# The delta rule's substitution columns: from SBUF to a PSUM bank

## The chip, the cores and the metric

The kernel runs on one core of one Trainium2 chip. The metric is the device time of one execution in microseconds, from the first to the last instruction, and less is better. Five engines work on their own instruction queues and wait for each other by semaphores: TensorE (PE), VectorE (DVE), ScalarE (ACT), GpSimd (POOL) and SyncE (SP), which issues most transfers. PE's results go to PSUM, eight banks of 512 fp32 words on each of 128 partitions. SBUF is the large working memory, and weights come from HBM.

## What is computed

The reference is a model of two layers on 512 tokens of width 1024. Each layer has a mixer and an expert stage (32 experts, two for each token). The first layer's mixer holds a linear recurrence and gated linear attention; the second layer's mixer, where the change lies, is a gated delta rule with eight heads of width 128. Its core is a triangular solve for each chunk, which is then followed by a recurrence over the chunks:

```
decay = exp(where(incl, gcum[:, None] - gcum[None, :], -inf))
k_beta = k * beta
lower = where(strict, einsum('id,jd->ij', k_beta, k) * decay, 0)
rhs = concat([v * beta, k_beta * exp(gcum)])
sol = triangular_solve(lower, rhs, unit_diagonal=True)
u, w = split(sol)
# recurrence: v_new = u - w @ state; o = q' @ state + att @ v_new
```

The reference takes chunks of 64 tokens. The kernel takes blocks of 128 tokens and builds the inverse of each unit lower triangular matrix once.

## The kernel before

**Stages.** One program runs through the first layer's mixer, its expert stage, the second layer's mixer (about 810 to 1215 us of the span) and its expert stage. In the mixers PE multiplies activations by weight blocks of 1 MB. Each weight block is split into a rounded part (`whi`, by ACT, L423) and a rest (`wlo`, by POOL, L424), and three products (L430 to L432) go into one bank of PSUM.

**The mixer with the delta rule** (`mixer_c`). The eight heads go in four groups of two. For each group, units "k", "q", "v" and "z" are projected; the units "o" are output projections. Each projected unit goes on by itself, as a generator that gives way for a number of steps: `keys` convolves (L1013, three DVE instructions on a PSUM bank and an SBUF tile), applies Silu on ACT (L1014), turns the result with PE, and makes the decay-weighted products `LT` (L1064). `queries` sums squares (POOL `sq` L1073, DVE `xt` L278 and `xr` L280, PE L284) and multiplies (L1082, L1083). `values` turns and scales (L1095, L1097).

**The solve.** When both heads of a group have their keys, `solve` starts. Its first part inverts all 32x32 diagonal blocks of the group at once, and it is the part that is touched. ACT gathers the blocks (`Ld`, four copies, L1107), DVE transposes them so that each partition holds one matrix (`Ll`, L1109) and scales them (L1112). `Yl` starts as a copy of the unit columns `y0` (L1114, POOL), which are made once. Then come 31 steps, each with one product and one difference on DVE: `tm = Yl column x Ll column` (L1119) and `Yl = Yl - tm` (L1121). Each difference needs the product before it and each product needs the difference before it, so the 62 instructions are one chain; they have 8 to 76 elements per partition. At the end `Yl` is transposed back into `Yt` (L1123), from which `X` (ACT, L1130) and `XT` (DVE, L1129) are filled. After a number of steps the blocks are joined with PE (L1138 to L1165), and `recurrence` (L1185 to L1213) uses the inverse.

**Order.** A planner behind the program sorts each engine's queue by the order of the program and by the time at which it reckons an instruction can start, so the substitution's instructions lie between convolutions, scalings and the recurrence's instructions on DVE. Each queue then runs in order. Tiles of PSUM come from one pool of eight (`ps`, one bank each), and a tile is given back when its last reader is done. `Yl` has one buffer of its own in SBUF (`ep`, `bufs=1`), so a group's copy waits for the group before.

Of the kernel before, what the change touches and what calls it, by code (L numbers as in the profile page):

```python
# [7 lines left out]
F32 = mybir.dt.float32  # L8
# [3 lines left out]
AF = mybir.ActivationFunctionType  # L12
# [5 lines left out]
P = 128  # L18
# [71 lines left out]
class Build:  # L90
# [829 lines left out]
    def mixer_c(self, u, es, right, second):  # L920
        tc, nc, a, st = self.tc, self.nc, self.a, self.stream
        C = self.C
        ep = self.pool(es, "ce")
# [18 lines left out]
        y0 = ep.tile([P, 8, 32], F32, name="y0")  # L942
# [80 lines left out]
        def keys(h, hd, p, g):  # L1023
# [43 lines left out]
            if g.nk == HG:  # L1067
                st.spawn(solve(g), 0)
# [31 lines left out]
        def solve(g):  # L1100


            LT = g.LT
            sb = [slice(32 * b, 32 * b + 32) for b in range(4)]
            Ld = ep.tile([P, 32, U], F32, name="Ld", bufs=1)
            for b in range(4):
                nc.scalar.activation(Ld[sb[b]], LT[sb[b], :, sb[b]].rearrange("p u i -> p i u"), AF.Copy)  # L1107
            Ll = ep.tile([P, 32, 32], F32, name="Ll", bufs=1)
            nc.vector.transpose(Ll.rearrange("p i j -> p (i j)"), Ld[:, :, None, :].to_broadcast([P, 32, 4, U]))  # L1109
            sl = ep.tile([P, 32], F32, name="sl", bufs=1)  # L1110
            nc.vector.transpose(sl, g.s[:, None, :].to_broadcast([P, 4, U]))
            nc.vector.tensor_mul(Ll, Ll, sl[:, :, None].to_broadcast([P, 32, 32]))  # L1112
            Yl = ep.tile([P, 8, 32], F32, name="Yl", bufs=1)
            nc.gpsimd.tensor_copy(Yl, y0)  # L1114
            tm = wk.tile([P, 256], F32, name="ltmp", tag="Pm", bufs=1)
            for s in range(31):
                n, c = 31 - s, s // 4 + 1
                tv = tm[:, :c * n].rearrange("l (c r) -> l c r", r=n)
                nc.vector.tensor_mul(tv, Yl[:, :c, s:s + 1].to_broadcast([P, c, n]),  # L1119
                                     Ll[:, s + 1:, s].rearrange("p (o r) -> p o r", o=1).to_broadcast([P, c, n]))  # L1120
                nc.vector.tensor_sub(Yl[:, :c, s + 1:], Yl[:, :c, s + 1:], tv)  # L1121
            Yt = ep.tile([P, 32, U], F32, name="Yt", bufs=1)
            nc.vector.transpose(Yt.rearrange("p c u -> p (c u)"), Yl.rearrange("p c r -> p (c r)"))  # L1123
            yield g.wait
            while g.i > self.solved:
                yield 1
            for b in range(4):
                src = Yt[sb[b]].rearrange("p c u -> p u c")
                nc.vector.transpose(XT[sb[b], :, sb[b]], src)  # L1129
                nc.scalar.activation(X[sb[b], :, sb[b]], src, AF.Copy)  # L1130
            yield 1

            lo32 = slice(0, 32)
            pP = self.ps([P, U, 32])
            for i in range(U):
                for b in range(2):
                    lo, hi = slice(64 * b, 64 * b + 32), slice(64 * b + 32, 64 * b + 64)
                    nc.tensor.matmul(pP[hi, i], LT[lo, i, hi], X[lo, i, lo], start=True, stop=True)  # L1138
            Pm = wk.tile([P, U, 64], F32, name="Pm", tag="Pm", bufs=1)
            for b in range(2):  # L1140
                hi = slice(64 * b + 32, 64 * b + 64)
                nc.vector.tensor_mul(Pm[hi, :, lo32], pP[hi], g.s[hi, :, None].to_broadcast([32, U, 32]))
            yield 2
            pX = self.ps([P, U, 32])
            for i in range(U):
                for b in range(2):
                    lo, hi = slice(64 * b, 64 * b + 32), slice(64 * b + 32, 64 * b + 64)
                    nc.tensor.matmul(pX[hi, i], XT[hi, i, hi], Pm[hi, i, lo32], start=True, stop=True)
                    nc.tensor.matmul(pX[lo, i], Pm[hi, i, lo32], XT[hi, i, hi], start=True, stop=True)
            for b in range(2):  # L1150
                lo, hi = slice(64 * b, 64 * b + 32), slice(64 * b + 32, 64 * b + 64)
                nc.vector.tensor_scalar(X[hi, :, lo], pX[hi], -1.0, None, op0=OP.mult)
                nc.scalar.activation(XT[lo, :, hi], pX[lo], AF.Copy, scale=-1.0)
            yield 2

            lo, hi = slice(0, 64), slice(64, 128)
            pP = self.ps([P, U, 64])
            for i in range(U):
                nc.tensor.matmul(pP[hi, i], LT[lo, i, hi], X[lo, i, lo], start=True, stop=True)
            nc.vector.tensor_mul(Pm[hi], pP[hi], g.s[hi, :, None].to_broadcast([64, U, 64]))  # L1160
            yield 2
            pX = self.ps([P, U, 64])
            for i in range(U):
                nc.tensor.matmul(pX[lo, i], Pm[hi, i], XT[hi, i, hi], start=True, stop=True)
            nc.scalar.activation(XT[lo, :, hi], pX[lo], AF.Copy, scale=-1.0)  # L1165
            if g.i == 0:
                self.dump("XT", XT)
            yield 2
            yield from recurrence(g)
            self.solved += 1  # L1170
# [817 lines left out]
```

## Time and profile before

| | |
|---|---|
| median of 3 runs | 1734.37 us (1732.44 to 1738.6) |
| the profiled execution | 1732.64 us, its span 1730.8 us |
| PE busy | 1636.0 us, 95% |
| PE's weight loads (beside PE) | 980.7 us, 57% |
| DVE busy | 797.8 us, 46% |
| ACT busy | 520.9 us, 30% |
| POOL busy | 397.2 us, 23% |
| mean transfer rate over the span | 286 GB/s read from HBM, of which the expert stages' main parts reach 413 GB/s |
| mean granted TensorE clock | 0.975 |

Busy shares are means over stages with different limits, so the page alone doesn't say what bounds the mixer with the delta rule. For that the trace is asked by stretch: who waited for whom, which instructions ran in order of time on each engine, and how long one instruction of a line took at least, at the median and at most. An instruction that takes much longer than others of its own shape was held by something while it ran.

### The profile page before, as it was taken

The page shows a single profiled execution, that of the slowest core. Times are in us where ns is not written, and L with a number is a line of the kernel's source. Part 1 is how long each engine was busy: PE and PEld are TensorE (multiplying, and loading weights), DVE is VectorE, ACT ScalarE, POOL GpSimd, SP SyncE. Part 2 cuts the span into 40 slices and gives each one's busy share as a digit, 9 for nine tenths or more (in the row PEclk, how much of TensorE's full clock was granted, in tenths as well). Part 3 has the DMA queues.
Part 4 walks back from the last instruction along what each step waited for, and adds up shares of the span by engine and source line. Part 5 has one row for each costly group of instructions (what it writes and reads, how often), then busy time and mean ns, then how long its engine had stood idle before and what let it go on. Part 6 is the DMA issues. An engine that isn't in the chain of part 4 may idle for free. (4 is left out here: it accounts for less than half of the span.)

```text
span 1730.8 us, 23035 instructions
## 1 busy us (share of the span) xinstructions
PE 1636.0 (95%) x8890; PEld 980.7 (57%) x8890; DVE 797.8 (46%) x1770; ACT 520.9 (30%) x1029; POOL 397.2 (23%) x350
## 2 busy tenths in 40 slices
PE   6999998899999999998988989899899999999996
PEld 3666667444455455454666666678544555455453
DVE  3346452433324243325688687865433324243324
ACT  4755323210111111015636466364310111111013
POOL 2454432210101001011434343453210001001011
PEclk9999998999999999998999999999999999999998
DMA  8665745689999999994243433136699999999992
GB/s 302 225 222 169 268 147 189 269 343 380 414 411 413 412 411 414 412 407 122 73 145 114 134 98 116 55 139 252 252 379 383 414 411 413 412 412 413 412 406 101
DMA packets 156561, 496.02 MB, mean 287 GB/s; under 512 B 16472, under 2 KB 43668, under 8 KB 141088
## 3 DMA queue, kind: packets, MB, share of 16 engines
q1 hardware_dynamic: 155488, 493.23, 74.1%
q8 instruction: 72, 1.18, 0.3%
q10 hardware_dynamic: 960, 1.28, 0.2%
q14 instruction: 41, 0.34, 0.1%
HBM read 492.21 MB, written 2.10 MB: 286 GB/s over the span
## 5 line engine op out<-in xcount | busy, mean ns | idle before, releaser
L1530 PE MATMUL ps<-w,XTm 128*64 128x512 f32 x2048 | 447.1, 593 | 0.6 <-DVE XTm L1459 0.6
L1530 PEld LDWEIGHTS ps<-w,XTm 128*64 128x64 f32 x2048 | 161.6, 137 | 268.3 <-issue 260.0
L424 POOL TENSOR_TENSOR wlo<-w,whi 128x512 fp32r<-128x512 f32 x136 | 184.6, 1363 | 243.8 <-ACT whi L423 224.9
L1584 PE MATMUL ps<-w,hT 128*64 128x512 f32 (+1 forms) x1056 | 230.8, 587 | 1.0 <-ACT hT L1562 1.0
L1553 DVE TENSOR_TENSOR gg<-gg,ps 128x512 f32<-128x512 f32 x32 | 22.0, 688 | 377.8 <-PE ps L1530 377.7
L430 PE MATMUL ps<-w,whi 128*128 128x512 f32 x384 | 165.0, 430 | 0.0
L431 PE MATMUL ps<-w,whi 128*128 128x512 f32 x384 | 155.5, 405 | 1.6 <-POOL w L554 1.2
L1584 PEld LDWEIGHTS ps<-w,hT 128*64 128x64 f32 x1056 | 82.2, 137 | 130.1 <-issue 117.4
L432 PE MATMUL ps<-w,wlo 128*128 128x512 f32 x384 | 155.8, 406 | 0.0
L1607 DVE TENSOR_TENSOR w<-w,ps 128x512 f32<-128x512 f32 (+1 forms) x248 | 149.2, 662 | 7.0 <-PE ps L1598 5.5
L1539 POOL CAST sel<-ident 32x128 fp32r<-32x128 f32 x32 | 9.0, 280 | 591.3 <-PE ps L1567 533.9
L1588 POOL TENSOR_TENSOR yl<-y,yh 128x512 fp32r<-128x512 f32 x60 | 76.5, 1275 | 251.2 <-ACT yh L1587 251.2
L1587 ACT ACTIVATE yh<-y 128x512 fp32r<-128x512 f32 (+1 forms) x66 | 40.8, 618 | 295.2 <-DVE y L1586 294.2
L423 ACT ACTIVATE whi<-w 128x512 fp32r<-128x512 f32 x136 | 84.5, 627 | 140.2 <-PE ps L431 69.1
L1454 PE MATMUL ps<-Dm,hhi 128*128 128x256 f32 x512 | 125.5, 287 | 0.0
L1454 PE MATMUL ps<-Dm,hlo 128*128 128x256 f32 x512 | 123.4, 283 | 0.0
L1586 DVE SCALAR_TENSOR_TENSOR y<-ps,wsl,gate 128x512 f32<-128x512 f32 (+1 forms) x66 | 48.5, 734 | 151.1 <-issue 76.4
L1454 PEld LDWEIGHTS ps<-Dm,hhi 128*128 128x128 f32 x512 | 101.1, 198 | 13.5 <-issue 13.4
L1598 PE MATMUL ps<-yh,dt 128*128 128x512 f32 (+1 forms) x264 | 106.0, 406 | 0.0
L1562 ACT ACTIVATE hT<-ps 128x512 f32<-128x512 f32 x32 | 19.1, 598 | 284.5 <-PE ps L1560 275.4
L1454 PEld LDWEIGHTS ps<-Dm,hlo 128*128 128x128 f32 x512 | 101.2, 198 | 0.0
L1598 PE MATMUL ps<-yl,dt 128*128 128x512 f32 (+1 forms) x264 | 100.9, 387 | 0.0
(522 smaller groups left out, 2383.5 us busy)
## 6 DMA issues: line engine op xcount, KB each, us to landing
w<-in_moe_w_dram SPq DMA_DIRECT2D x380, 1024.0 KB
w<-in_w_ada_dram SPq DMA_DIRECT2D x40, 1024.0 KB
w<-in_w_in_c_dram SPq DMA_DIRECT2D x16, 1024.0 KB
w<-in_w_in_ab_dram SPq DMA_DIRECT2D x10, 1024.0 KB
wst<-in_w_ada_dram SPq DMA_DIRECT2D x8, 1024.0 KB
w<-in_w_out_ab_dram SPq DMA_DIRECT2D x4, 1024.0 KB
w<-in_moe_w_dram SPq DMA_DIRECT2D x8, 512.0 KB
w<-in_w_out_c_dram SPq DMA_DIRECT2D x4, 1024.0 KB
```

The source lines that it names most:

```text
L423: nc.scalar.activation(hi, src, AF.Copy)
L424: nc.gpsimd.tensor_sub(lo, src, hi.bitcast(F32))
L430: mm(p, lhs[0], rhs[0], start=start, stop=False)
L431: mm(p, lhs[0], rhs[1], start=False, stop=False)
L432: mm(p, lhs[1], rhs[0], start=False, stop=stop)
L1454: nc.tensor.matmul(p, spread(src[:, t], k // 4)[k % 4], Dm[:, t].rearrange("p e s -> p (e s)"), start=t + i == 0, stop=t == NT - 1 and i == 1)
L1530: self.nc.tensor.matmul(ps[j][half[e]], X[:, k, half[e]], w, start=k == 0, stop=k == KD - 1)
L1584: nc.tensor.matmul(py[half[e]], hT[:, k, half[e]], w, start=k == 0, stop=k == 3)
L1586: nc.vector.scalar_tensor_tensor(y32, py, wsl, gate[:, c], op0=OP.mult, op1=OP.mult)
L1588: (nc.vector if last else nc.gpsimd).tensor_sub(yl[:, c], y32, yh[:, c].bitcast(F32))
L1598: mm = nc.tensor.matmul(p, dt[:, t * P:(t + 1) * P], y[:, s], start=i == 0, stop=i == 1)
L1607: nc.vector.tensor_add(h, h, p)
```

## The change

`Yl` becomes a tile of the PSUM pool, and its first content is written by ACT instead of POOL. All later instructions stay as they are in the code, but read and write `Yl` in PSUM.

```diff
             nc.vector.transpose(sl, g.s[:, None, :].to_broadcast([P, 4, U]))
             nc.vector.tensor_mul(Ll, Ll, sl[:, :, None].to_broadcast([P, 32, 32]))
-            Yl = ep.tile([P, 8, 32], F32, name="Yl", bufs=1)
-            nc.gpsimd.tensor_copy(Yl, y0)
+
+            Yl = self.ps([P, 8, 32])
+            nc.scalar.activation(Yl, y0, AF.Copy)
             tm = wk.tile([P, 256], F32, name="ltmp", tag="Pm", bufs=1)
             for s in range(31):
                 n, c = 31 - s, s // 4 + 1
```

`self.ps` takes a whole bank of 512 words and gives a view of the first 256.

## Rows read from the trace of the kernel before

**Rows 1.** The page, part 1: busy us, share of the span, instructions.
```profile
PE 1636.0 (95%) x8890; PEld 980.7 (57%) x8890; DVE 797.8 (46%) x1770; ACT 520.9 (30%) x1029; POOL 397.2 (23%) x350
```

**Rows 2.** PE's waits, 860 to 1135 us: us in total, times, longest.
```profile
PE ps L284 <- DVE xr L280: 5.2, 3, 3.3
PE ps L1095 <- ACT vT L1014: 5.1, 3, 3.2
PE ps L284 <- DVE Yl L1121: 3.1, 1, 3.1
...
PE ps L1029 <- ACT kT L1014: 2.8, 1, 2.8
```

**Rows 3.** Groups by line, 780 to 1200 us: busy us, mean ns | idle before.
```profile
L1119 DVE TENSOR_TENSOR ltmp<-Yl,Ll 128x60 f32<-128x60 f32 (+24 forms) x124 | 44.2, 356 | 2.5
L1121 DVE TENSOR_TENSOR Yl<-Yl,ltmp 128x60 f32<-128x60 f32 (+24 forms) x124 | 41.2, 332 | 2.5
```

**Rows 4.** Single lines, whole span: ns min/median/max, first to last start.
```profile
L1119 DVE TENSOR_TENSOR ltmp<-Yl,Ll x124: 163/265/1396, 867.8 to 1127.0; 128x60 f32<-128x60 f32 x12, 128x28 f32<-128x28 f32 x8, 128x54 f32<-128x54 f32 x8, 128x48 f32<-128x48 f32 x8
L1121 DVE TENSOR_TENSOR Yl<-Yl,ltmp x124: 155/215/1335, 868.1 to 1128.1; 128x60 f32<-128x60 f32 x12, 128x28 f32<-128x28 f32 x8, 128x54 f32<-128x54 f32 x8, 128x48 f32<-128x48 f32 x8
L1064 DVE TENSOR_TENSOR LT<-ps,E x8: 675/685/693, 854.5 to 1085.1; 128x512 f32<-128x512 f32 x8
L1045 DVE TENSOR_TENSOR ksc<-brk,ex x8: 151/976/978, 850.6 to 1083.0; 128x4 f32<-128x4 f32 x8
L1114 POOL COPY Yl<-y x4: 396/397/397, 815.7 to 1057.3; 128x256 f32<-128x256 f32 x4
L1000 DVE COPY ex<-ps x1: 182/182/182, 842.8 to 842.8; 128x32 f32<-128x32 f32 x1
L989 DVE COPY gd<-gd x1: 180/180/180, 840.7 to 840.7; 128x32 f32<-128x32 f32 x1
L1038 PE MATMUL ps<-grow,pick x8: 490/494/792, 846.0 to 1075.3; 40*128 40x512 f32 x8
```

**Rows 5.** DVE's timeline in the first group: start us, us, instruction.
```profile
868.75 1.00 DVE L1119 TENSOR_TENSOR ltmp<-Yl,Ll 128x29 f32<-128x29 f32 x1
869.79 1.18 DVE L1121 TENSOR_TENSOR Yl<-Yl,ltmp 128x29 f32<-128x29 f32 x1
871.00 1.20 DVE L1119 TENSOR_TENSOR ltmp<-Yl,Ll 128x28 f32<-128x28 f32 x1
...
872.34 0.70 DVE L278 STREAM_TRANSPOSE xt<-sq 128x512 f32<-128x512 f32 x1
```

**Rows 6.** POOL's timeline in the same stretch; three instructions, the first and last here.
```profile
868.65 1.04 POOL L1073 TENSOR_TENSOR sq<-qT 128x512 f32<-128x512 f32 x1 [1.95 <-ACT qT L1014]
...
870.88 1.26 POOL L424 TENSOR_TENSOR wlo<-w,whi 128x512 fp32r<-128x512 f32 x1
```

**Rows 7.** The expert stage by windows: PE, PEld, DVE, ACT, POOL, PEclk, DMA, GB/s.
```profile
1400.00:1500.00 100.00, 100.00 (x518) 52.83 (x518) 34.48 (x62) 11.89 (x20) 8.79 (x10) 1.00 1.02 413
```

**Rows 8.** ACT's groups by line and shape, 780 to 1200 us.
```profile
L916 ACT ACTIVATE ychi<-yf 128x256 fp32r<-128x256 f32 x16 | 6.6, 414 | 21.4 <-DVE yf L915 21.4
...
L1053 ACT ACTIVATE E<-E 128x512 f32<-128x512 f32 x8 | 5.0, 626 | 0.0
L1056 ACT ACTIVATE qg<-ps 128x512 f32<-128x512 f32 x8 | 4.7, 591 | 0.1
```

**Rows 9.** Five windows of PE at a low clock: us, busy, PEclk, DMA, GB/s.
```profile
873.40:880.20 6.80, 6.28 (x22) 0.50 0.29 111
...
sum 20.40, PE 19.63; mean PE 3.93
```

**Rows 10.** Timelines in the third group: two output tiles' first matmuls, the last reader.
```profile
1016.48 0.48 PE L430 MATMUL ps<-whi,ychi 128*128 128x512 f32 x1
...
1022.49 0.73 PE L430 MATMUL ps<-whi,ychi 128*128 128x512 f32 x2
...
1034.69 0.68 DVE L530 TENSOR_TENSOR w<-w,ps 128x512 f32<-128x512 f32 x1
```

## The prediction

> **What bounds the kernel now.** The profiled execution took 1732.64 us, of which its span is 1730.8; the median of the three runs, 1734.37, lies 1.7 above it. I read the busy times first: PE is busy for 95% of the span [rows 1]. So a change to DVE counts only where PE waits for DVE. The touched code runs between 868 and 1128 us, in the delta rule of the second layer. I therefore read PE's waits from 860 to 1135 us [rows 2]. The reader is to see two things there. No wait is for a PSUM bank: each names a producer. And all but the weight transfer (2.8), the split on POOL (0.6) and two ACT results (qT 1.0, XT 0.6) end in a DVE result, or in an ACT result (vT, kT) made right behind DVE convolutions. These waits sum to 22.0 us, in twelve rows of which the first four stand here; the other eight have 0.2 to 1.4 each.
>
> Next I asked why DVE is late there. The substitution is 124 products (L1119) and 124 differences (L1121), 85.4 us in all [rows 3]. Their means are 356 and 332 ns, but their medians are 265 and 215 ns [rows 4], so a few are very long. The timeline shows which: an instruction on 29 elements takes 1.00 us, the next two 1.18 and 1.20, just while POOL runs three tensor products back to back [rows 5, 6]. Counted row by row against the shortest of the same shape, 37 of the 248 are longer by more than 0.15 us, and each of the 37 overlaps a POOL instruction. The excess is 7.1, 5.8, 7.6 and 9.3 us in the four groups, 29.8 us together; means less medians give nearly that, 124 x (91 + 117) ns = 25.8 us.
>
> Which DVE instructions are held? One that takes one tensor from PSUM and one from SBUF is not: LT (L1064) on 512 elements spans 675 to 693 ns [rows 4]. One that takes both from SBUF is: ksc (L1045), on 4 elements, is 151 ns at best and 976 at the median [rows 4]. Today all 248 are of the second kind. With Yl in PSUM, each product reads Yl from PSUM and Ll from SBUF, each difference Yl from PSUM and ltmp from SBUF: all become the first kind.
>
> [...]
>
> After 1230 us the expert stage keeps PE busy 100 us of 100 while the transfers run at 413 GB/s [rows 7]. Its loads wait for room that the mixer's last PE and POOL work frees, so I let time saved in the mixer move the end one for one.
>
> **The change part by part.** *POOL loses four copies* of 397 ns [rows 4]. POOL sits idle before nearly all of its work, so I count nothing; if they matter it is a gain of at most 1.6 us. POOL's queue no longer stands behind a copy that waits for the previous group's result.
>
> *ACT gains four copies* into PSUM. An ACT activation on 128x256 takes 414 ns [rows 8]; the table need not change, since the same function already runs between the others. The input y0 has been there since 815 us, so nothing new is waited for but a bank. The cover is the 2.5 us in which DVE transposes and scales Ll behind ACT's Ld. Cost zero; uncovered, 4 x 0.41 = 1.7 us. Behind the copy on ACT stand splits of weights (whi) and Silu; PE would wait for those if the copy waited long for a bank.
>
> *The price of PSUM per DVE instruction.* Reading it costs nothing visible: a copy of 32 elements out of PSUM takes 182 ns, one out of SBUF 180 [rows 4]. No DVE instruction of the trace writes PSUM, and none reads and writes the same bank. I bound it by rows that are far: ACT reading 512 elements from PSUM needs 591 ns against 626 from SBUF [rows 8], so -35 ns; and the product costs 50 ns more than the difference (265 against 215 ns at the median [rows 4]), an access less regular by a stride, so +50 ns. I take +10, nearest to the two copies. On 248 instructions that is 2.5 us of DVE, between -8.7 and +12.4.
>
> [...]
>
> *What PE gets back.* The single waits are read off PE's timeline; their sums by cause are [rows 2]. For each I followed DVE back to its last idle moment and summed the excess on the way; a wait shrinks by no more than that.
> First group: waits 3.15 (L284) and 0.6 (vT). Excess 2.83 before the first, 7.1 before the second. xt (872.34) can't start before POOL's sq ends, 868.65 + 1.04 = 869.69 [rows 5, 6], so 2.6 + 0.6 = 3.2 us.
> Second group: five waits, 1.05 + 0.51 + 1.49 + 1.16 + 0.24 = 4.45 us, against 3.33 of excess: 3.3 us.
> Third group: 3.30 + 0.59, against 3.2: 3.0 us, the same limit by sq. Later the kT wait, 2.75, against 4.05: 2.75 us.
> Fourth group: 1.29 + 3.25 + 1.44 + 0.37 = 6.35, against 8.5: 6.3 us.
> Sum 18.6; about 145 instructions lie in these chains, at +10 ns 1.5 us, of which 0.6 bind: 18.
>
> *The clock.* [...] Since residues of 0.6 to 1 us stay in the first and third groups I take 8.
>
> *What it costs.* Yl holds one of eight banks from its copy to Yt, 25 to 36 us in each group. In groups one, two and four I count, tile by tile from first matmul to last reader, at most six live banks; there it is free. In the third, four outputs of the output projection wait from 1016.5 to 1022.8 us for DVE, and the last is read at 1034.69 [rows 10]. Together with recurrence tiles that makes seven or eight live banks for 8.8 us, all eight for 3.9. One less costs PE between 0 and 8.8 us, and DVE, faster by then, drains earlier: I take 2. If copies were pulled ahead as far as POOL's are (35 to 54 us), banks would be gone twice as long. Against that, eight matmuls (L1038) that lacked only a bank were issued in pairs over 229 us, not at once [rows 4].
>
> *What is late next:* sq on POOL, the w_ada load (2.55 us at 975.6, longer if PE comes earlier), and whatever another order of the queues makes late. I take 4 us.
>
> Sum: 18 + 8 - 2 - 4 = 20 us less. 1730.8 - 20 + 1.84 = 1712.6 for the profiled kind of run, **1714** for the median.
>
> **The rivals.** *A fixed price at the upper bound, +50 ns.* The chains then give 2.9 + 1.7 + 2.4 + 2.2 + 4.9 = 14 us, the clock some 5, less 6: 13, so 1721. Its upside twin, no residue anywhere, gives 21.7 + 9.8 = 31.5: 1703.
>
> *The banks eat it.* The third group loses all 8.8 us and a fall of the clock, 3.4: 20 + 2 - 12 = 10 us gained, 1724. For it: [rows 10]. Against it: PE has other work whose banks are taken already.
>
> *The change doesn't do what it says:* DVE is still held, by what it writes or by Ll alone. Gain 0, banks cost 2: 1736. Against it stand the eight LT rows without a single long one.
>
> *Slower: writing PSUM in a dependent chain.* Every difference waits for the product before it and every product for the difference. If a result in PSUM shows late to the next instruction, each step pays. It decides at 29.8 us / 248 = 120 ns per instruction, where the excess is paid back. At 200 ns DVE gets 49.6 us longer and 19.8 net; by the chains above, +1.3 in group four (49 x 0.2 - 8.5), +3.3 for kT, +3.3 in group two, some 3 in group one, 11 in all: 1745. For it: no row of before prices such a write. Against it: the reads cost 2 ns.
>
> **How the numbers follow.** Forecast 1714, with chance 0.50; the fixed price (1721) 0.20; no residue (1703) 0.05; banks (1724) 0.07; no effect (1736) 0.08; slow writes (1745) 0.10. A measurement of this kernel tells 0.3%, 5.2 us, from no change. Faster by more than that would be 0.82, from the first four; I move 0.02 of it to no change, for orders of the queues that I can't see, and 0.02 to slower, for banks held long. So faster 0.78, same 0.08 + 0.02 = 0.10, slower 0.10 + 0.02 = 0.12. The range reaches from no residue to no effect, 1702 to 1738, and leaves out slow writes and the tails, under 0.2.
>
> **What would show it.** In the changed profile L1119 and L1121 should have no instruction over 0.45 us while POOL runs, and their sum should fall from 85.4 to about 58 us. That sum being above 85 means slow writes; long ones among the 248 still overlapping POOL mean no effect. PE's waits for xr, Yl, kT, vT and vb should fall from some 14 us to 4, and the stretches at 0.50 near 873, 1034, 1064, 1112 and 1119 us should mostly be gone. A PE wait ended by a DVE reader of a bank (L530, L1013), or an ACT wait before the Yl copy, means banks. The expert stage should look the same, only earlier. If DVE is freed by 25 us and the mixer still ends where it did, my step from DVE to PE is wrong.

## The result and the profile after

The change took the time from 1735.69 us (median of six runs) to 1716.22 us, a ratio of 0.9885 with the interval 0.9868 to 0.9902. The forecast was 1714, in a range of 1702 to 1738. The profiled execution of the changed kernel took 1716.33 us and its span 1714.6, against 1732.64 and 1730.8: 16.2 us of span to be found. In the new file every line behind L1114 has moved by one: the product is L1120, the difference L1122, ACT's copy L1115.

First the page, part 1 (busy us, share of the span, instructions), to set beside [rows 1]:

```profile
PE 1630.9 (95%) x8890; PEld 979.8 (57%) x8890; DVE 766.4 (45%) x1770; ACT 522.6 (30%) x1033; POOL 396.1 (23%) x346
```

DVE lost 31.4 us of busy time with the same 1770 instructions. Here are the groups by line, as in [rows 3]:

```profile
L1120 DVE TENSOR_TENSOR ltmp<-ps,Ll 128x60 f32<-128x60 f32 (+24 forms) x124 | 29.3, 236 | 2.4
L1122 DVE TENSOR_TENSOR ps<-ps,ltmp 128x60 f32<-128x60 f32 (+24 forms) x124 | 26.5, 214 | 2.3
```

And the single lines (ns min/median/max, first to last start), as in [rows 4]:

```profile
L1120 DVE TENSOR_TENSOR ltmp<-ps,Ll x124: 154/245/297, 868.7 to 1109.0; 128x60 f32<-128x60 f32 x12, 128x28 f32<-128x28 f32 x8, 128x54 f32<-128x54 f32 x8, 128x48 f32<-128x48 f32 x8
L1122 DVE TENSOR_TENSOR ps<-ps,ltmp x124: 163/218/246, 868.9 to 1109.4; 128x60 f32<-128x60 f32 x12, 128x28 f32<-128x28 f32 x8, 128x54 f32<-128x54 f32 x8, 128x48 f32<-128x48 f32 x8
...
L1115 ACT ACTIVATE ps<-y x4: 361/370/388, 856.3 to 1072.5; 128x256 f32<-128x256 f32 x4
```

The reader is to look at the maxima. 1396 and 1335 ns have become 297 and 246; the sum of the 248 instructions is 55.8 us where it was 85.4. The medians hardly moved: 245 against 265, and 218 against 215. So nothing got faster; the long ones went. The stretch of [rows 5, 6] shows it best, DVE's timeline first and POOL's behind it (start, length):

```profile
869.36 0.20 DVE L1122 TENSOR_TENSOR ps<-ps,ltmp 128x30 f32<-128x30 f32 x1
869.59 0.20 DVE L1120 TENSOR_TENSOR ltmp<-ps,Ll 128x29 f32<-128x29 f32 x1
869.83 0.20 DVE L1122 TENSOR_TENSOR ps<-ps,ltmp 128x29 f32<-128x29 f32 x1
870.56 0.71 DVE L278 STREAM_TRANSPOSE xt<-sq 128x512 f32<-128x512 f32 x1 [0.54 <-POOL sq L1073]
```

```profile
869.49 1.04 POOL L1073 TENSOR_TENSOR sq<-qT 128x512 f32<-128x512 f32 x1 [1.95 <-ACT qT L1014]
870.49 1.28 POOL L1079 TENSOR_TENSOR qg<-qg,qT 128x512 f32<-128x512 f32 x1
871.72 1.29 POOL L424 TENSOR_TENSOR wlo<-w,whi 128x512 fp32r<-128x512 f32 x1
```

The same POOL product sq runs, and beside it the instructions on 29 elements that took 1.00 and 1.18 us now take 0.20 each. In the whole trace 105 of the 248 lie beside a POOL instruction and none is over 0.3 us; before, 61 did, and 37 of them were over 0.45 us. What such an instruction waits for is seen in the trace of before: each of the 37 started while a POOL instruction ran, and ended 0.02 to 0.16 us after that POOL instruction did (in [rows 5, 6], sq ends at 869.69 and the first long one at 869.75; wlo at 872.14 and the third at 872.20). Of the 24 that were not held, 19 had started before the POOL instruction beside them. So these holds lasted as long as what was left of POOL's instruction, to within 0.16 us. The bracket in DVE's fourth line is the new limit: xt waits for sq itself.

PE's waits from 860 to 1135 us (us in total, times, longest), to set beside [rows 2], all that have 0.5 or more:

```profile
PE ps L284 <- DVE xr L280: 3.7, 5, 1.2
PE ps L911 <- ACT orow L907: 2.4, 2, 1.9
PE ps L1139 <- ACT X L1131: 2.3, 2, 2.0
PE ps L1195 <- DVE rr__7207 L1188: 1.6, 1, 1.6
PE ps L258 <- DMA w<-in_w_ada_dram: 1.1, 2, 0.8
PE ps L1186 <- DVE w L530: 1.0, 2, 0.8
PE ps L1195 <- DVE rr__7294 L1188: 1.0, 1, 1.0
PE ps L1082 <- ACT qT L1014: 1.0, 1, 1.0
PE ps L303 <- DMA modst<-modrow: 0.8, 1, 0.8
```

The waits for vT (5.1), Yl (3.1), kT (2.8) and vb (1.4) are gone. But new ones have come: L911 for orow, L1139 for X, L1186 for a bank that DVE (L530) frees, and 0.8 us at L303 for a transfer (modst). All of PE's waits in this stretch came to 27.0 us before and come to 16.6 now, 10.4 less. The clock: six stretches at 0.50 (23.9 us; five are in [rows 9], the sixth is the first line here) have become three (13.6 us, the lines behind it), by windows (length, PE busy, PEld, DVE, ACT, POOL, granted clock, DMA, GB/s):

```profile
975.80:979.20 3.40, 3.40 (x14) 1.57 (x7) 0.79 (x3) 1.21 (x3) 1.98 (x2) 0.50 0.20 26
```

```profile
1021.90:1028.70 6.80, 6.04 (x19) 4.87 (x19) 5.15 (x23) 0.78 (x3) 0.01 (x1) 0.50 0.03 8
1062.80:1066.20 3.40, 3.40 (x13) 1.02 (x9) 1.12 (x2) 2.54 (x8) 1.28 (x1) 0.50 0.22 31
1127.70:1131.10 3.40, 3.40 (x12) 2.71 (x11) 0.83 (x3) 1.76 (x8) 1.56 (x2) 0.50 0.00 0
```

Half of the 10.3 us less at 0.50 is 5.1 us, an estimate from the granted shares of 0.50 and 1.00, and so is each half of such a time below. In the trace of before, matmuls on 512 columns (L430 to L432) that follow each other without idle time start 427 ns apart at 0.50 and 232 at 1.00 (medians; 978.24 and 978.67 us, against 968.19 and 968.42), which would make it 4.7. With the waits the half gives 15.5 of the 16.2 us. From the start of the last norm's warm-up matmuls to the end the two traces are alike, 513.8 and 513.7 us: what the mixer gains moves the end one for one.

### The profile page after: what moved, and what is told of

Same layout as the page of the kernel before. It is cut to its first block, busy times and chain, and to the rows that moved or that the text cites. A ratio compares the mean times of both kernels' runs of the same rounds, so it can differ in the third digit from the quotient of the medians.

```text
span 1714.6 us, 23030 instructions
## 1 busy us (share of the span) xinstructions
PE 1630.9 (95%) x8890; PEld 979.8 (57%) x8890; DVE 766.4 (45%) x1770; ACT 522.6 (30%) x1033; POOL 396.1 (23%) x346
## 3 DMA queue, kind: packets, MB, share of 16 engines
q8 instruction: 72, 1.18, 0.3%
## 5 line engine op out<-in xcount | busy, mean ns | idle before, releaser
L430 PE MATMUL ps<-w,whi 128*128 128x512 f32 x384 | 162.9, 425 | 0.7 <-ACT w L552 0.7
L432 PE MATMUL ps<-w,wlo 128*128 128x512 f32 x384 | 154.1, 402 | 0.0
```

What stands on the lines that cost most here:

```text
L430: mm(p, lhs[0], rhs[0], start=start, stop=False)
L432: mm(p, lhs[1], rhs[0], start=False, stop=stop)
```

## The experiments

The theory: a DVE instruction that reads two SBUF tensors is held while POOL runs a tensor instruction; Yl in PSUM leaves each of the 248 with one SBUF input; the freed DVE time reaches PE as shorter waits and as a clock that doesn't fall. Its rivals: the copy's move from POOL to ACT does it; or the order of the engines' queues, which the planner makes anew for every program (by the lists of both orders, 109 of DVE's 1139 instructions there stand elsewhere in the changed kernel; an expectation below says 64 places); or DVE's mere busy time counts, not the holds; and the bank costs something.

**The copy alone.** Yl stays in SBUF, ACT copies.

```diff
-            nc.gpsimd.tensor_copy(Yl, y0)
+            nc.scalar.activation(Yl, y0, AF.Copy)
```

> Yl stays in SBUF; only its first copy moves from POOL to ACT. If the gain of the change comes from DVE instructions that no longer read two SBUF tensors (theory 1), all 248 are still held: the sum of products and differences stays near 85 us and the time near 1735 us (ratio to before 0.998 to 1.002). If the gain comes from POOL's queue losing its copies, or from another order of the queues (theory 2), the time falls to about 1716 to 1725 us with the sum still near 85.

Measured: 1736.35 us, ratio 0.9997 [0.9986, 1.0009]; the substitution takes 84.8 us. The move of the copy is worth nothing.

**Half of the change, the other tensor.** ltmp goes to PSUM, Yl stays in SBUF: the products still read two SBUF tensors, the differences one.

```diff
-            tm = wk.tile([P, 256], F32, name="ltmp", tag="Pm", bufs=1)
+            tm = self.ps([P, 256])
```

> Yl stays in SBUF with its POOL copy; ltmp goes to a PSUM bank instead, held for as long as Yl's was. The products still read two SBUF tensors, the differences read one from SBUF and one from PSUM. Theory 1: products keep their long instructions (mean about 356 ns, longest about 1.4 us), differences lose theirs (mean about 215, longest under 0.3 us). The excess of before is 11 to 15 us in the differences, so DVE gets 11 to 15 us back and the time falls by about half of the change's 19: 1723 to 1729 us. If a write to PSUM or a bank were what helps or costs (theory 3), products, which write PSUM here, would change as much as differences.

Measured: 1738.79 us, ratio 1.0014 [1.0005, 1.0023]. The single lines:

```profile
L1119 DVE TENSOR_TENSOR ps<-Yl,Ll x124: 174/274/1361, 867.6 to 1118.6; 128x60 f32<-128x60 f32 x12, 128x28 f32<-128x28 f32 x8, 128x54 f32<-128x54 f32 x8, 128x48 f32<-128x48 f32 x8
L1121 DVE TENSOR_TENSOR Yl<-Yl,ps x124: 145/206/235, 867.8 to 1118.8; 128x60 f32<-128x60 f32 x12, 128x28 f32<-128x28 f32 x8, 128x54 f32<-128x54 f32 x8, 128x48 f32<-128x48 f32 x8
```

The mechanism came out as expected: products up to 1361 ns, differences never above 235, 73.4 us in all. What counts here is the inputs: the products, with two from SBUF, are held though they write PSUM. But the time did not follow, and PE has single waits of 8.7 us for vT, 6.0 for rr and 5.2 for Yl, where none was over 3.3 before. The expectation failed. Either freed DVE time is worth nothing here, or something else changed with it. The queues had: ltmp no longer shares its buffer with Pm, and their order is another. So the order had to be held fixed.

**The order of e2 without its tensor in PSUM.** The file of before, its instructions queued on PE, DVE, ACT and POOL in e2's order. Here and below the order is given as a list for each engine, each instruction queued behind the one ahead of it in the list:

```diff
         Build(tc, args, outs[0]).build()
+        fix_order(nc, tc, ORDER)
```

> The kernel before, nothing in PSUM, with the instructions on PE, DVE, ACT and POOL in the order that e2_ltmp_in_psum had. Theory 1: e2 took 12 us of holds away and paid as much for a worse order, so the same order with all holds is slower than e2's 1738.8: 1743 to 1753 us. Theory 2 (DVE time freed from holds is worth little in any order): 1736 to 1741 us.

Measured: 1748.24 us, ratio 1.0068 [1.0046, 1.0091]. Its waits, the three longest:

```profile
PE ps L1095 <- ACT vT L1014: 10.7, 2, 9.2
PE ps L1194 <- DVE rr__7203 L1187: 6.0, 1, 6.0
PE ps L1194 <- DVE rr__8074 L1187: 5.1, 1, 5.1
```

These are e2's waits, now with no operand moved: they belong to the order. It costs 12.6 us, and ltmp in PSUM gave 9.5 of them back (1748.24 to 1738.79), with 79.9 us of substitution becoming 73.4.

**Both orders, both places of Yl.** The first kernel is the changed kernel's order on all four engines with Yl in SBUF, copied by ACT. The second is the changed kernel with PE and DVE in the order of before; ACT's and POOL's order was left to the planner there, and by the traces it isn't that of before.

> Yl in SBUF again, copied there by ACT, so the 248 instructions read two SBUF tensors as before; but every instruction of the second layer's mixer stands on PE, DVE, ACT and POOL in exactly the order of the changed kernel, which differs from that of the kernel before in 64 places on DVE. Theory 1 (the held instructions alone made the difference): 1730 to 1738 us, the substitution's sum near 85 us. Theory 2 (the other order of the queues made it): 1714 to 1721 us, though the sum is near 85. If both do a part, the time lies between and shows the parts.

> The changed kernel, Yl in PSUM, but with PE's and DVE's instructions of that stretch in the order of the kernel before. Theory 1 (holds): 1714 to 1722 us, substitution near 56 us. Theory 2 (order): 1730 to 1738 us, substitution near 56 us all the same.

Measured: 1737.71 us, ratio 1.0008 [0.9994, 1.0022], and 1708.48 us, ratio 0.9849 [0.9823, 0.9874]. The first time is as theory 1 expects, though its sum is 89.0 us and not near 85; the second lies 5.5 us below the 1714 to 1722 of theory 1, so that expectation missed on the fast side. Groups by line, first the one with Yl in SBUF, then the one with Yl in PSUM:

```profile
L1119 DVE TENSOR_TENSOR ltmp<-Yl,Ll 128x60 f32<-128x60 f32 (+24 forms) x124 | 49.2, 397 | 2.4
L1121 DVE TENSOR_TENSOR Yl<-Yl,ltmp 128x60 f32<-128x60 f32 (+24 forms) x124 | 39.8, 321 | 2.3
```

```profile
L1120 DVE TENSOR_TENSOR ltmp<-ps,Ll 128x60 f32<-128x60 f32 (+24 forms) x124 | 29.3, 236 | 2.5
L1122 DVE TENSOR_TENSOR ps<-ps,ltmp 128x60 f32<-128x60 f32 (+24 forms) x124 | 26.5, 214 | 2.5
```

| order of the queues | Yl in SBUF | Yl in PSUM | gain |
|---|---|---|---|
| of before (with Yl in PSUM: PE and DVE only) | 1735.67 | 1708.48 | 27.2 |
| of the changed kernel | 1737.71 | 1716.22 | 21.5 |

This settles the main question. In the changed kernel's order, the same on all four engines in both kernels, Yl's place alone makes 21.5 us; the new order by itself is no gain at all (ratio 1.0008). In the profiled executions of that pair PE's waits from 860 us to the last norm fall from 30.6 to 16.6 us, and the stretches at 0.50 from 34.3 to 13.6 us: 14.0 us and half of 20.7 are 24.3 of the 24.4 us between the spans. The row of before agrees, though its 27.2 us may hold a part that is ACT's and POOL's order. With Yl in PSUM the new order is a loss of 7.7 us. Where that loss lies is seen in PE's waits of the kernel in the old order, the same stretch and view as above:

```profile
PE ps L284 <- DVE xr L280: 4.0, 5, 1.5
PE ps L1195 <- DVE rr__7207 L1188: 1.8, 1, 1.8
PE ps L430 <- ACT orow L907: 1.4, 1, 1.4
PE ps L1082 <- ACT qT L1014: 1.0, 1, 1.0
PE ps L258 <- DMA w<-in_w_ada_dram: 1.0, 1, 1.0
```

No wait for X, none for the bank of L530, and orow at 1.4 and 0.6 us where the changed kernel has 2.4. All its waits come to 14.4 us, and there is no stretch at 0.50 between 860 and 1135 us. The windows 860 to 1190 us, first of before, then of the changed kernel, then of this one (length, PE, PEld, DVE, ACT, POOL, granted clock, DMA, GB/s):

```profile
860.00:1190.00 330.00, 302.67 (x2007) 229.36 (x2000) 258.62 (x686) 181.16 (x389) 139.89 (x121) 0.96 0.38 126
```

```profile
860.00:1190.00 330.00, 313.22 (x2106) 240.88 (x2105) 238.44 (x701) 190.07 (x408) 141.39 (x122) 0.98 0.42 141
```

```profile
860.00:1190.00 330.00, 315.47 (x2151) 242.67 (x2152) 239.66 (x704) 190.42 (x415) 141.71 (x122) 1.00 0.42 143
```

The trace has 2007, 2106 and 2151 matmuls in the same 330 us, at a clock of 0.96, 0.98 and 1.00. Between the last two, 2.2 us of waits and half of 13.6 us at the low clock are 9.0 us; the spans differ by 7.4. X (2.8 us) and the bank of L530 (1.7) stand in the new order's variant with Yl in SBUF too: they are the order's, not PSUM's.

**DVE time without holds.** The changed kernel with each product made twice, first in an order that the planner makes for it, then in the changed kernel's own order with the second product right behind the first.

```diff
-                nc.vector.tensor_mul(tv, Yl[:, :c, s:s + 1]...
+                for _ in range(2):
+                    nc.vector.tensor_mul(tv, Yl[:, :c, s:s + 1]...
```

> The changed kernel with each of the 124 products made twice in a row: about 124 x 0.25 = 30 us more DVE work in the same chains, all of it free of POOL. Theory 1 says that DVE's time in these chains is what counts: the 30 us that the change freed are put back, and the time returns to between 1728 and 1740 us. If DVE's time there were hidden, and the gain came from order or from POOL, it stays below 1722.

> The changed kernel with each product made twice as in e4_product_twice, but every other instruction kept in the changed kernel's own order, the second product right behind the first. DVE again has some 29 us more to do than in the changed kernel, now with no order found around it. If e4 stayed at 1724.4 because the order was found anew with that time in view: 1730 to 1740 us. If 29 us spread evenly over the substitution cost PE less than the same time in a few long holds: 1721 to 1727 us.

Measured: 1724.44 us, ratio 0.9934 [0.9919, 0.9949], and 1727.64 us, ratio 0.9962 [0.9943, 0.9980]. The products of the second:

```profile
L1121 DVE TENSOR_TENSOR ltmp<-ps,Ll 128x60 f32<-128x60 f32 (+24 forms) x248 | 59.0, 238 | 6.6
```

So 29.7 us of DVE work, as much as the holds had been, cost 8.2 us where the order was made around it and 11.4 where it was not. The first expectation (1728 to 1740) missed; the second lies 0.6 us above its lower case. In the same order 33.2 us of holds (89.0 less 55.8) cost 21.5. That is 0.38 us of time for each us of even load, and 0.65 for each us of holds. Part of that has another source: the kernel with holds waits 4.0 us for the w_ada transfer, the one with products twice not at all, and why that load comes later isn't shown.

**The bank by itself.** The kernel before, with a bank taken by ACT's copy of y0 and held until DVE reads it behind the substitution.

```diff
+            hold = self.ps([P, 8, 32])
+            nc.scalar.activation(hold, y0, AF.Copy)
...
+            nc.vector.tensor_copy(tm[:, 0:8], hold[:, :, 0])
```

> Before, with Yl and its work in SBUF as they were, and beside it one PSUM bank written by ACT ahead of each substitution and read by one small DVE copy after it: the price of the bank alone. My forecast had 2 us for it, bounds 0 to 8.8, all in the third group: 1735 to 1745 us, middle 1738. If the bank costs nothing: within 0.2% of before. A PE wait ended by a DVE reader of a bank (L530) near 1020 to 1035 us would show it.

Measured: 1735.96 us, ratio 0.9992 [0.9981, 1.0003]. A bank held that long costs nothing that could be measured here. The queues were not held to the order of before, and DVE's is another in the trace, so a small price could be hidden by what that order gives; against it stands that the changed kernel in PE's and DVE's old order has no wait for a bank either.

**More POOL work.** Eight POOL products more in each group, in the kernel before and in the one with Yl in PSUM, PE and DVE in the old order in both. The result of the added work isn't used.

```diff
+            junk = ep.tile([P, 256], F32, name="junk", bufs=1)
+            lf = Ll.rearrange("p i j -> p (i j)")
+            for _ in range(8):
+                nc.gpsimd.tensor_mul(junk, lf[:, :256], lf[:, 512:768])
```

> The kernel before, its PE and DVE order kept, with eight more POOL products of 128x256 (each some 0.75 us, 5.9 us per group, their result used nowhere) that start when Ll is ready, so beside the substitution. If POOL's tensor work is what holds a DVE instruction with two SBUF inputs: the sum of the substitution rises from 85 us by 10 to 24 us (at most the 24 us of added POOL work) and the time to 1742 to 1765 us. If the long instructions come from something else (transfers, ACT, PE), the sum stays within 3 us of 85.

> The same eight POOL products per group in the changed kernel, Yl in PSUM, PE and DVE in the order of the kernel before (e6_psum_in_old_order: 1708.5 us). If one SBUF input frees DVE from POOL: the substitution stays at 55 to 57 us, none over 0.45 us; the time rises only by what POOL's own later work (the split wlo) costs: 1708 to 1722 us. If DVE is held all the same by denser POOL work: above 65 us.

Measured: 1745.33 us, ratio 1.0054 [1.0037, 1.0071], and 1719.83 us, ratio 0.9898 [0.9879, 0.9917]. The added POOL work and the substitution, first with Yl in SBUF, then in PSUM:

```profile
L1123 DVE TENSOR_TENSOR ltmp<-Yl,Ll 128x60 f32<-128x60 f32 (+24 forms) x124 | 45.4, 366 | 2.5
L1125 DVE TENSOR_TENSOR Yl<-Yl,ltmp 128x60 f32<-128x60 f32 (+24 forms) x124 | 48.8, 394 | 2.5
L1118 POOL TENSOR_TENSOR junk<-Ll 128x256 f32<-128x256 f32 x32 | 24.0, 751 | 4.1 <-DVE Ll L1112 1.2 <-DVE or L901 1.2
```

```profile
L1124 DVE TENSOR_TENSOR ltmp<-ps,Ll 128x60 f32<-128x60 f32 (+24 forms) x124 | 29.2, 236 | 2.5
L1126 DVE TENSOR_TENSOR ps<-ps,ltmp 128x60 f32<-128x60 f32 (+24 forms) x124 | 26.5, 214 | 2.5
L1119 POOL TENSOR_TENSOR junk<-Ll 128x256 f32<-128x256 f32 x32 | 23.4, 732 | 4.1 <-DVE or L901 1.2 <-DVE Ll L1112 1.2
```

With Yl in SBUF, instructions over 0.45 us rise from 37 to 62, each beside POOL, and the sum from 85.4 to 94.2: 8.8 us, just under the 10 that were expected at least. Each of the 62 again ends 0.02 to 0.14 us after the POOL instruction in which it started. With Yl in PSUM the sum is 55.7, and of 161 instructions beside POOL none is over 0.3 us. That is the mechanism, turned up from POOL's side. The times say less, since both kernels lost about as much (9.8 and 11.4 us). In the second, PE waits for xr instead (9.3 us, the longest 5.0): xt stands behind sq, and sq on POOL now behind the added products.

**What is left of the holds.** The kernel with Yl in PSUM in the old order, with more DVE work of two SBUF inputs taken off DVE. The edit moved L1043; the expectations name L1045, which lies two lines on and stayed on DVE.

```diff
-            nc.vector.tensor_mul(sc[:, 1], sc[:, 0], ehat[:, :, h])
+            nc.gpsimd.tensor_mul(sc[:, 1], sc[:, 0], ehat[:, :, h])
...
-            nc.vector.scalar_tensor_tensor(rr, ss, 1.0 / P, eq, op0=OP.mult, op1=OP.add)
-            nc.scalar.activation(rr, rr, AF.Sqrt)
+            for h in range(n):
+                nc.scalar.activation(rr[:, h:h + 1], ss[:, h:h + 1], AF.Sqrt, scale=1.0 / P, bias=eq[:, h:h + 1])
```

> A version meant to beat both: Yl in PSUM, the order of the kernel before on PE and DVE, and the two other lines with DVE instructions that POOL holds taken off DVE: the 4-element product of L1045 goes to POOL, and L899 with its square root becomes one ACT square root per head with scale and bias. In the changed kernel these two lines were held for 4.9 and 4.3 us. If what is left of such holds still reaches PE: 1700 to 1706 us. If PE's remaining waits don't hang on them: 1706 to 1711 us. If POOL's queue (L1045 behind its long products) or ACT's makes sc or the root late: 1711 to 1720 us.

> As e11, but only L1045's product moved to POOL, L899 as it was. Holds matter: 1702 to 1708 us; they don't: 1706 to 1711; POOL's queue makes sc late: above 1711. With e11 it tells the two lines apart.

Measured: 1711.43 us, ratio 0.9858 [0.9841, 0.9874], with both edits, and 1708.67 us, ratio 0.9845 [0.9829, 0.9862], with the first alone. The single line L1045, first in the kernel without these edits, then with the first:

```profile
L1045 DVE TENSOR_TENSOR ksc<-brk,ex x8: 152/975/980, 850.6 to 1068.2; 128x4 f32<-128x4 f32 x8
```

```profile
L1045 DVE TENSOR_TENSOR ksc<-brk,ex x8: 165/166/1064, 850.4 to 1067.0; 128x4 f32<-128x4 f32 x8
```

L1045 was freed all the same, from 975 to 166 ns at the median, since POOL, with L1043 ahead, begins its long product E in five of the eight only 0.07 or 0.08 us after L1045 has started. The time did not move (1708.48 and 1708.67): the holds of L1045 don't reach PE. For those of L899 it isn't shown, since the second edit also gave ACT more to do. It made the kernel 2.8 us slower; its longest PE wait is one of 3.6 us for rr (L1195), where the other has 1.8.

## Why the prediction was right, and where its sum was not

*The mechanism.* All 248 instructions were to be freed, no instruction over 0.45 us, a sum of about 58 us. They were; the sum is 55.8, and the added POOL work shows that POOL is the cause.

*The price of PSUM*, taken at +10 ns with bounds of -35 and +50. The excess was 29.8 of the 85.4 us, so 55.6 would be left at no price at all; 55.8 is a price of (55.8 - 55.6) / 248, about 1 ns. Shape by shape, against the instructions of before that lay beside no POOL work, the median product takes 7 ns less in PSUM and the median difference 7 ns more (means over 25 shapes); the two cancel. The two copies of [rows 4], which differ by 2 ns, were the right rows; the slow-writes rival falls with them. Beside POOL none of 105 instructions with one SBUF input is held, and 37 of 61 with two are.

*PE's waits*, 18 us. They fell by 10.4. In PE's and DVE's old order they fell by 12.6, so this term was too large in itself: I followed each wait to the whole excess behind it, but the waits for xr only went from 5.2 to 3.7, since xt then waits for sq on POOL (4.6 us of DVE's waits, against 1.6; DVE's waits from 860 to 1135 us, first of before, then of the changed kernel):

```profile
DVE xt L278 <- POOL sq L1073: 1.6, 3, 1.0
```

```profile
DVE xt L278 <- POOL sq L1073: 4.6, 6, 1.5
```

I had taken that limit for two groups; it shows in more. My "some 14 us" for the five named waits was also an error of addition: the rows give 5.2 + 5.1 + 3.1 + 2.8 + 1.4 = 17.6, and the changed kernel has 3.7 of them. The 21.7 us of the upside twin is 21.2 by the waits listed for the four groups, which moves that case by half a microsecond.

*The clock*, 8 us, and 9.8 in the upside twin. No run shows these two terms: they were my estimates. What the traces show is 10.3 us less at 0.50 in the changed kernel, and none of the 23.9 us left in the old order; by half of that the clock gave 5.1 and 12 us, by the starts of the matmuls 4.7 and 10.9. I had counted five stretches [rows 9]; the sixth, of 3.4 us at 975.8, went too. So waits and clock together are 24.6 us where PE's and DVE's order is kept, against my 26: the sum was right, its split was not.

*The banks*, 2 us, with a bound of 8.8: nothing measurable by itself, with the order left to the planner. The bank wait of L530 that I named as its sign did appear, 1.0 us, but it stands in the same order with Yl in SBUF too.

*What is late next*, 4 us. This was the mis-sized term. I had sq, the w_ada load and "another order of the queues" in it. With Yl in PSUM the order is 7.7 us, more than my losses together, and nothing in the trace of before could size it. That the forecast came within 2.2 us of the result is in part luck: losses of 2 for banks and 4 for the rest add to 6, near the 7.7 that the order took, though I had them for other reasons.

*ACT's copies and POOL's*, nothing: right (0.9997). ACT's take 370 ns, under the 414 I had as their row, and no table load stands at their line, L1115 (L1014 has 15, of 1283 ns each). *The end of the kernel moves one for one:* right, 513.8 and 513.7 us.

## What to carry to other kernels

Where many small DVE instructions with two SBUF inputs run beside POOL's tensor work, look at their maxima, not at their means: a median of 265 and a maximum of 1396 ns at one line were holds here, since the long ones ended within 0.16 us of a POOL instruction, and one operand in PSUM removed them (maximum 297 ns) at no price that the time of these runs could show. Before you judge such an edit, look whether the order of the queues moved with it, and measure old and new in one order: here three orders of the same work lay at 1735.7, 1737.7 and 1748.2 us. The version with Yl in PSUM and PE's and DVE's old order, with L1043 on POOL, is faster than both kernels: 0.9845 [0.9829, 0.9862] against 0.9885 [0.9868, 0.9902]; without L1043's move the ratio is 0.9849 [0.9823, 0.9874].

## What the runs showed of the hardware

The DVE products that read one operand from PSUM were not dearer than those that read both from SBUF (medians 245 and 265 ns), and the chain in which each product reads what the difference before it wrote to the bank ran at 0.24 us a step (starts 869.36, 869.59 and 869.83). A held DVE instruction waited for the end of the POOL instruction that ran when it started: all 37 in the kernel before, and all 62 with more POOL work, end 0.02 to 0.16 us after it. POOL was slower too, though less: its 128x256 product takes 751 ns on the mean beside DVE with two SBUF inputs (six of 32 take 810 to 860) and 732 beside DVE with one (none over 745). And microseconds of DVE were not alike: 29.7 us of even extra work cost 8 to 11 us, 33.2 us of holds 21.5.
